# Two-layer hybrid encoder step on one core: the feed-forward stages take the first token group by itself, then the other two together, and the state-space input product opens with three blocks

## The chip, the cores and the metric

The kernel is one program on one core of a Trainium2 chip. The metric is the device time of one execution in microseconds (us), as the median of several runs. The core has a matmul engine (TensorE, PE in the profile, with its weight loads as PEld), three engines for elementwise work (VectorE, DVE; ScalarE, ACT; GpSimd, POOL), and SyncE (SP), which here only issues DMA transfers. Each engine runs its own list of instructions in order.

## The reference

1024 prompt tokens and 32 sample tokens pass through two layers in float32. Layer 0 mixes tokens by retention and forgetting attention, attends to 256 memory tokens, and ends in a feed-forward stage; layer 1 has a state-space mixer (S5) in place of the first step and then the same two. Every part is wrapped in norms:

```python
x = x + rmsnorm(part(rmsnorm(x) * w_pre)) * w_post
```

The feed-forward part, which the change rewrites, is

```python
h = relu(x @ w_up) ** 2      # 1024 -> 4096
y = h @ w_down               # 4096 -> 1024
```

and the S5 part begins with a product 1024 -> 1024 (`winc` in the kernel).

## The kernel before

Activations lie with features on the 128 partitions and tokens along the free axis. The 1056 tokens are three groups: 0 and 1 of 384 tokens, 2 of 288. A weight block is 128 outputs by 1024 inputs (512 KB).

**Products.** Each float32 product is three passes over exact splits of both sides, x = hi + lo and w = hi + lo (`mm3`): hi·hi, hi·lo, lo·hi. One block for one group is 8 inputs by 3 passes, 24 matmuls into one PSUM bank; three banks take turns (tag `mm`). All matmuls are recorded on line L72.

**Weights.** `wload` brings a block into `wst` (two buffers) by a DMA on the SP queue (L135), ScalarE copies it to `wh` (L139) and VectorE subtracts to get `wl` (L140); `wh` and `wl` have four buffers each. An optional offset gives these two a higher place in the order.

**Order of work.** The matmul engine's list is laid out by hand: `po.later(d, fn)` puts a piece off until d microseconds of products stand before it, and `po.tick()` lets due pieces in. The lists of the other engines are made by a scheduler from priorities; `tc.high_priority(offset=HP)` moves work ahead. Within `gemm` the evacuations of a block run in such a region.

**Feed-forward.** `mlp` goes over the 4096 hidden features in 8 chunks of 4 blocks. For each chunk it loads 4 up blocks, computes them for group 0, then 1, then 2 (`gemm`, evacuation `evac_up`: relu on ScalarE L1343, square on VectorE L1344, `ho` high part on ScalarE L1346, low part on GpSimd L1347), loads 4 down blocks, and adds the 8 outputs of each group to `Y` (first chunk a copy by ScalarE, then VectorE L1366). In the last chunk a group's outputs are squared and summed (`sumsq`: ScalarE L244, GpSimd L245) and `done(g)` starts the group's `update`. The third up block of the first chunk alone is loaded with the high offset HP.

**Update.** `update` closes each part for one group: the sums of squares become reciprocal norms (piece `c` on the matmul engine, put off by 3.2 us of products, then a broadcast `b`, put off by 3.0 us more), then for each of 8 feature tiles VectorE scales (`upd`, L273), adds the residual `xr` (L274; GpSimd takes some of them), ScalarE makes the high split `xh` (L201) and VectorE the low split `xl` (L202), and ScalarE squares it for the next norm (L244, added by GpSimd at L245). The next part's product for the group needs the splits of all 8. `r` is what the next stage scales its outcome by.

**What lies ahead of the change.** The output product of the memory attention ends with group 2 as well; its updates for groups 1 and 2 still run when the feed-forward begins with group 0. The end of layer 0's feed-forward meets the S5 input product in the same way; that product takes 2 blocks for all groups and then one block at a time (`gran`), and its states and outputs (`s5_block`) are put between the products by `po.later`.

Of the kernel before, what the change touches and what calls it, by code (L numbers as in the profile page):

```python
"""Hybrid retention / forgetting-attention / S5 streaming step on one core.

Activations are feature-major: features on partitions, tokens along the free axis; the 1024 prompt
tokens and the 32 sample tokens share every weight (token groups of 384, 384 and 256 + 32).
Large float32 products run as three float32r passes over exact splits x = hi + lo, w = hi + lo
(hi*hi + hi*lo + lo*hi); small products run in float32.
"""
# [9 lines left out]
F32 = mybir.dt.float32  # L17
F32R = mybir.dt.float32r
AF = mybir.ActivationFunctionType
# [4 lines left out]
NG = (384, 384, 288)  # L24
# [7 lines left out]
class _Order:  # L32
    """The tensor engine's program is laid out piece by piece; a piece that waits for other engines
    is put off until enough other products stand before it."""
# [29 lines left out]
def _body(tc, A):  # L64
# [21 lines left out]
    with es:  # L86
# [17 lines left out]
        # ---------------- constants  # L104
# [22 lines left out]
        # ---------------- helpers  # L127
# [20 lines left out]
        # evacuations can be held back until the pool they write to may be opened  # L148
# [14 lines left out]
        def gemm(blocks, load, rhs, evac, gran, done=None, post=None, lead=0, final=(0, 1, 2)):  # L163
            """blocks of 128 outputs, gran at a time for each token group; the first `lead` advance together"""
# [39 lines left out]
        def rstd_cols(acc, nt, scale, half=False, r=None, tag="rc", ps=None):  # L204
            """acc: [128, nt*128] partial sums of squares by partition -> [128, nt] reciprocal rms.
            With r, the columns summed up still lack a factor r^2."""
# [40 lines left out]
        def update(o, g, ys, acc, gpost, xres, xout, last=False, row=False, scale=1.0 / 1024, half=False, r=None):  # L247
            """x + rmsnorm(y) * g; o gets the split of the new x times the next norm's gain, and its
            reciprocal rms by token, in columns or along a row of all partitions"""
# [71 lines left out]
        # ---------------- memory keys and values of a layer (prompt)  # L321
# [63 lines left out]
        # ---------------- state-space layer: discretisation and per-group chunk matrices  # L385
# [8 lines left out]
        def s5_prepare(sp):  # L394
# [10 lines left out]
            # angles lambda_im*dt * (1, 8, 16, ..., 512), reduced to [-pi, pi]  # L405
# [20 lines left out]
            # powers a^0..a^8  # L426
# [19 lines left out]
            # input gains  # L446
# [26 lines left out]
            def group(f):  # L473
# [20 lines left out]
                def cmul(xr, xi, pr, pi, n, nm, neg):  # L494
                    """outer products over (power, channel): real part and (negated) imaginary part"""
# [839 lines left out]
        def mlp(l, X, done):  # L1335
            Y = [[None] * 8 for _ in range(3)]
            for c in range(8):
# [14 lines left out]
                for g in range(3):  # L1352
                    acc = acc_tile(NG[g]) if c == 7 else None
                    for o in range(8):
# [6 lines left out]
                        with tc.high_priority(offset=HP):  # L1361
# [5 lines left out]
                            if c == 7:  # L1367
                                sumsq(acc, Y[g][o], NG[g], o == 0, "sqa")
# [325 lines left out]
```

## Time and profile before

| what | value |
|---|---|
| device time, three runs | 3298.2, 3298.15, 3295.02 us; median 3298.15 us |
| span of the profiled execution | 3296.3 us |
| matmul engine busy | 3160.3 us (96%) |
| VectorE, ScalarE, GpSimd busy | 45%, 33%, 28% of the span |
| weight loads (`wh`, `wl`) | 252 |

The runs list no separate time for the profiled execution; its span is 1.85 us under the median of the runs. A wait of the matmul engine counts, a wait of another engine only where the matmul engine waits for it in turn. In the profile an arrow names the engine and line whose result ended an idle stretch. The granted clock is a share of full speed: 1.0 stands for 2.4 GHz and 0.5 for 1.2 GHz.

### The profile page before, as it was taken

Reading aid. Unit: us, or ns where it says so; the run is one execution under the profiler, and the core shown is the slowest. Engines: PE = TensorE matmul, PEld = TensorE weight load, DVE = VectorE, ACT = ScalarE, POOL = GpSimd, SP = SyncE. Lnnn points to the kernel's source line nnn. Section 1 sums busy time; section 2 is a strip of 40 time slices with the busy share of each in tenths; the row PEclk is TensorE's granted clock in tenths of the full one; section 3 lists DMA queues with packets and bytes.
Section 4 is the critical chain, followed back from the end, with each engine's and each line's share of the span. In section 5 each row is a group of like instructions: output and inputs, shape, how many; then the busy total and the mean of one; then the engine's idle time right before and its main releaser. Section 6 shows DMA issues by size and latency. Waiting matters only on the chain.

```text
span 3296.3 us, 50246 instructions
## 1 busy us (share of the span) xinstructions
PE 3160.3 (96%) x19972; PEld 3059.2 (93%) x19972; DVE 1495.2 (45%) x2756; ACT 1071.6 (33%) x2117; POOL 914.5 (28%) x1182
## 2 busy tenths in 40 slices
PE   7999999998999999999999888998999999999997
PEld 7899986688999999999999878998999999999997
DVE  8843566527435223332334797227426132233224
ACT  5212335425435322221124334225435321222212
POOL 4873431216115211111114442015106111111115
PEclk9999999999999999999999998999999999999998
DMA  5562244124114211110112677114124110111113
GB/s 157 156 194 70 62 137 128 38 58 141 52 42 128 65 42 52 52 47 31 52 52 74 204 241 222 57 52 141 49 66 124 52 47 32 52 52 52 39 58 99
DMA packets 176336, 285.71 MB, mean 87 GB/s; under 512 B 34027, under 2 KB 130508, under 8 KB 175972
## 3 DMA queue, kind: packets, MB, share of 16 engines
q1 hardware_dynamic: 132310, 215.02, 21.8%
q10 hardware_dynamic: 35328, 41.83, 3.8%
q0 software_dynamic: 8464, 25.66, 2.3%
q8 instruction: 157, 2.57, 0.3%
q14 instruction: 77, 0.63, 0.1%
HBM read 220.17 MB, written 66.39 MB: 87 GB/s over the span
## 4 chain that ended last, share of the span: by engine, by line
PE 77%; DVE 7%; POOL 6%; DMA 4%; issue 4%; ACT 2%; SPq 0%; DVEq 0%; ACTq 0%; POOLq 0%
PE mm L72 68%; PE a L72 4%; PE b L72 2%; POOL q L527 2%; POOL acc L245 2%; PE c L72 1%; DVE xl L202 1%; DVE wl L140 1%; DVE upd L274 1%; POOL ET L528 1%; DMA ed<-ET 1%; POOL ET L529 1%; DVE upd L273 1%; PE b L76 1%; DMA mt<-in_memt_dram 0%
## 5 line engine op out<-in xcount | busy, mean ns | idle before, releaser
L72 PE MATMUL mm<-xh,wh 128*128 128x384 f32 (+1 forms) x3168 | 1050.4, 332 | 6.5 <-ACT mo L382 3.7
L72 PE MATMUL mm<-xh,wl 128*128 128x384 f32 (+1 forms) x3168 | 1031.4, 326 | 7.4 <-DVE wl L140 7.3
L72 PE MATMUL mm<-xl,wh 128*128 128x384 f32 (+1 forms) x3168 | 1031.9, 326 | 1.2 <-DVE xl L202 1.2
L72 PE MATMUL mm<-ho,wh 128*128 128x384 f32 (+1 forms) x3456 | 822.9, 324 | 1.5 <-DVE y L1366 1.5
L72 PEld LDWEIGHTS mm<-xh,wh 128*128 128x128 f32 x3168 | 603.5, 190 | 13.8 <-issue 5.0
L72 PEld LDWEIGHTS mm<-xh,wl 128*128 128x128 f32 x3168 | 602.4, 190 | 9.0 <-DVE wl L140 9.0
L72 PEld LDWEIGHTS mm<-xl,wh 128*128 128x128 f32 x3168 | 603.5, 190 | 1.8 <-DVE xl L202 1.8
L72 PEld LDWEIGHTS mm<-ho,wh 128*128 128x128 f32 x3456 | 603.5, 188 | 1.8 <-DVE y L1366 1.8
L72 PE MATMUL mm<-ho,wl 128*128 128x384 f32 (+1 forms) x1728 | 558.2, 323 | 0.0
L1347 POOL TENSOR_TENSOR ho<-u,ho 128x384 fp32r<-128x384 f32 (+1 forms) x192 | 183.3, 955 | 1176.2 <-ACT ho L1346 1150.4
L140 DVE TENSOR_TENSOR wl<-wst,wh 128x1024 fp32r<-128x1024 f32 (+1 forms) x252 | 318.5, 1264 | 416.0 <-ACT wh L139 412.8
L139 ACT ACTIVATE wh<-wst 128x1024 fp32r<-128x1024 f32 (+1 forms) x252 | 266.5, 1059 | 708.9 <-PE mm L72 641.6
L245 POOL TENSOR_TENSOR acc<-acc,sq 128x384 f32<-128x384 f32 (+2 forms) x259 | 280.9, 1093 | 412.1 <-ACT sq L244 406.5
L1366 DVE TENSOR_TENSOR y<-y,mm 128x384 f32<-128x384 f32 (+1 forms) x336 | 174.3, 519 | 353.4 <-PE mm L72 353.2
L72 PEld LDWEIGHTS mm<-ho,wl 128*128 128x128 f32 x1728 | 325.5, 188 | 0.0
L1344 DVE TENSOR_TENSOR u<-u 128x384 f32<-128x384 f32 (+1 forms) x192 | 103.3, 538 | 409.7 <-ACT u L1343 409.7
L1343 ACT ACTIVATE u<-mm 128x384 f32<-128x384 f32 (+1 forms) x192 | 88.0, 458 | 313.8 <-PE mm L72 313.6
L1346 ACT ACTIVATE ho<-u 128x384 fp32r<-128x384 f32 (+1 forms) x192 | 95.7, 498 | 172.1 <-DVE u L1344 172.1
L1206 POOL TENSOR_SCALAR p<-p,mx 128x256 f32<-128x256 f32 (+1 forms) x72 | 36.7, 510 | 241.4 <-DVE mx L1205 138.8
L202 DVE SCALAR_TENSOR_TENSOR xl<-upd,gall,xh 128x384 fp32r<-128x384 f32 (+1 forms) x120 | 100.0, 834 | 5.1 <-ACT xh L201 4.8
L244 ACT ACTIVATE sq<-y 128x384 f32<-128x384 f32 (+1 forms) x126 | 61.9, 495 | 109.7 <-DVE y L1366 56.2
L72 PE MATMUL mm<-xo,wh 128*128 128x384 f32 (+1 forms) x384 | 92.1, 324 | 0.0
(427 smaller groups left out, 4132.9 us busy)
## 6 DMA issues: line engine op xcount, KB each, us to landing
wst<-in_wup_dram SPq DMA_DIRECT2D x64, 512.0 KB
wst<-in_wdn_dram SPq DMA_DIRECT2D x64, 512.0 KB
xs<-upd ACTq DMA_DIRECT2D x80, 192.0 KB
xr<-xs SPq DMA_DIRECT2D x80, 192.0 KB
wst<-in_wab_dram SPq DMA_DIRECT2D x20, 512.0 KB
wst<-in_wxk_dram SPq DMA_DIRECT2D x16, 512.0 KB
wst<-in_wxv_dram SPq DMA_DIRECT2D x16, 512.0 KB
wst<-in_wxq_dram SPq DMA_DIRECT2D x16, 512.0 KB
```

The source lines that it names most:

```text
L72: return nc.tensor.matmul(out, lhsT, rhs, **kw)
L139: act(wh[:, :n], st[:, :n], AF.Copy)
L140: vtt(wl[:, :n], st[:, :n], wh[:, :n].bitcast(F32), op=SUB)
L202: stt(l, src, gain, h.bitcast(F32), op0=MULT, op1=SUB)
L244: act(sq[:, :n], src, AF.Square)
L245: return gtt(acc[:, :n], acc[:, :n], sq[:, :n], op=ADD)
L527: gtt(o[:, :, :, :m], ET[:, :, :, :m], a_, op=MULT)
L1343: act(t, ps, AF.Relu)
L1344: vtt(t, t, t, op=MULT)
L1346: act(h, t, AF.Copy)
L1347: gtt(lo, t, h.bitcast(F32), op=SUB)
L1366: vtt(Y[g][o], Y[g][o], ps, op=ADD)
```

## The change

`mlp` no longer calls `gemm`. It first takes group 0 alone through the whole feed-forward, in 4 chunks of 8 up blocks and 8 down blocks (each down block of 1024 hidden features by 128 outputs is now half of two loads), and calls `done(0)`. Then it takes groups 1 and 2 together in 8 chunks of 4, as before. Every up and down weight is therefore read and split twice: 64 more loads of 512 KB in each layer, 128 in all. The number of matmuls stays the same. `hidden`, which replaces `evac_up`, is not in a high-priority region, and no up weight is loaded with HP any more. In S5 the first pass of the input product takes 3 blocks for all groups in place of 2.

```diff
         def mlp(l, X, done):
+            def hidden(ps, g, new):
+                n = NG[g]
+                t = npl.tile([128, 384], F32, tag="tmp", bufs=2, name="u")[:, :n]
+                act(t, ps, AF.Relu)
+                vtt(t, t, t, op=MULT)
+                h, lo = new(), new()
+                act(h, t, AF.Copy)
+                gtt(lo, t, h.bitcast(F32), op=SUB)
+                return h, lo
+            def up(w, x, g):
+                ps = bank()[:, : NG[g]]
+                for k in range(8):
+                    s = slice(k * 128, k * 128 + 128)
+                    mm3(ps, w[0][:, s], w[1][:, s], x[k][0], x[k][1], k == 0, k == 7)
+                    po.tick()
+                return ps
+            def down(ws, H, o, g):
+                ps = bank()[:, : NG[g]]
+                for k in range(len(H)):
+                    wh, wl = ws[k // 4]
+                    s = slice((k % 4) * 256 + (o % 2) * 128, (k % 4) * 256 + (o % 2) * 128 + 128)
+                    mm3(ps, wh[:, s], wl[:, s], H[k][0], H[k][1], k == 0, k == len(H) - 1)
+                    po.tick()
+                return ps
+            def gather(Y, o, g, ps, first, acc):
+                with tc.high_priority(offset=HP):
+                    if first:
+                        Y[o] = ytile(g)
+                        act(Y[o], ps, AF.Copy)
+                    else:
+                        vtt(Y[o], Y[o], ps, op=ADD)
+                    if acc is not None:
+                        sumsq(acc, Y[o], NG[g], o == 0, "sqa")
             Y = [[None] * 8 for _ in range(3)]
+            x = get(X, 0)
+            for c in range(4):
+                H = []
+                for b in range(8):
+                    w = wload(A["wup"][l, 8 * c + b], 8)
+                    H.append(hidden(up(w, x, 0), 0, lambda: otile(0)))
+                acc = acc_tile(NG[0]) if c == 3 else None
+                for s4 in range(4):
+                    ws = [wload(A["wdn"][l, 2 * c + j, s4], 4) for j in range(2)]
+                    for o in (2 * s4, 2 * s4 + 1):
+                        gather(Y[0], o, 0, down(ws, H, o, 0), c == 0, acc)
+            done(0, Y[0], acc)
             for c in range(8):
-                H = [[None] * 4 for _ in range(3)]
-                def evac_up(b, g, ps):
-                    n = NG[g]
-                    t = npl.tile([128, 384], F32, tag="tmp", bufs=2, name="u")[:, :n]
-                    act(t, ps, AF.Relu)
-                    vtt(t, t, t, op=MULT)
-                    h, lo = otile(g), otile(g)
-                    act(h, t, AF.Copy)
-                    gtt(lo, t, h.bitcast(F32), op=SUB)
-                    H[g][b] = (h, lo)
-                gemm(range(4), lambda b: wload(A["wup"][l, 4 * c + b], 8, HP if c == 0 and b == 2 else 0), lambda g, k: get(X, g)[k], evac_up, 4)
+                H = {1: [], 2: []}
+                ws = [wload(A["wup"][l, 4 * c + b], 8) for b in range(4)]
+                for g in (1, 2):
+                    for b in range(4):
+                        H[g].append(hidden(up(ws[b], get(X, g), g), g, lambda: otile(g)))
                 ws = [wload(A["wdn"][l, c, s], 4) for s in range(4)]
-                for g in range(3):
+                for g in (1, 2):
                     acc = acc_tile(NG[g]) if c == 7 else None
                     for o in range(8):
-                        wh, wl = ws[o // 2]
-                        ps = bank()[:, : NG[g]]
-                        for k in range(4):
-                            s = slice(k * 256 + (o % 2) * 128, k * 256 + (o % 2) * 128 + 128)
-                            mm3(ps, wh[:, s], wl[:, s], H[g][k][0], H[g][k][1], k == 0, k == 3)
-                            po.tick()
-                        with tc.high_priority(offset=HP):
-                            if c == 0:
-                                Y[g][o] = ytile(g)
-                                act(Y[g][o], ps, AF.Copy)
-                            else:
-                                vtt(Y[g][o], Y[g][o], ps, op=ADD)
-                            if c == 7:
-                                sumsq(acc, Y[g][o], NG[g], o == 0, "sqa")
+                        gather(Y[g], o, g, down([ws[o // 2]], H[g], o, g), c == 0, acc)
                     if c == 7:
                         done(g, Y[g], acc)
...
         close_after(left, X, (0, 1), s5_start)
-        gemm(range(8), lambda b: wload(A["winc"][b], 8, HP if b < 2 else 0), lambda g, k: get(X, g)[k], evac_u, lambda at: 2 if at == 0 else 1,
+        gemm(range(8), lambda b: wload(A["winc"][b], 8, HP if b < 2 else 0), lambda g, k: get(X, g)[k], evac_u, lambda at: 3 if at == 0 else 1,
              post=lambda b, g: s5_block(b, uts.pop(b)) if un[b] == 3 else None, final=(2, 0, 1))
         mem = memory_k(1, 2)
```

The rest of the difference takes out comments.

**VectorE at the start of layer 0's feed-forward, before.** `wl_12046` belongs to the third up weight, and `upd`, `xl` and `xr` here to groups 1 (384 wide) and 2 (288 wide) of the update; `upd_12174` is the first instruction of group 2's.

```order
L140 TENSOR_TENSOR wl_12046<-wst_12043,wh_12045 128x1024
L202 SCALAR_TENSOR_TENSOR xl_12090<-upd_12086,gall_81,xh_12089 128x384
L273 SCALAR_TENSOR_TENSOR upd_12152<-y_11741,gall_81,b_11928 128x384
L1344 TENSOR_TENSOR u_12114<-u_12114 128x384
L202 SCALAR_TENSOR_TENSOR xl_12131<-upd_12127,gall_81,xh_12130 128x384
L274 TENSOR_TENSOR upd_12152<-upd_12152,xr_12150 128x384
L273 SCALAR_TENSOR_TENSOR upd_12174<-y_11357,gall_81,b_12166 128x288
```

The fourth weight's `wl_12052` follows 10 rows below, in the middle of group 2's update.

**The same place after.** `wl_12200`, `wl_12277` and `wl_12362` belong to the third, fourth and fifth up weight.

```order
L273 SCALAR_TENSOR_TENSOR upd_12377<-y_12026,gall_81,b_12154 128x288
L274 TENSOR_TENSOR upd_12377<-upd_12377,xr_12375 128x288
L202 SCALAR_TENSOR_TENSOR xl_12323<-upd_12319,gall_81,xh_12322 128x288
L202 SCALAR_TENSOR_TENSOR xl_12345<-upd_12341,gall_81,xh_12344 128x288
L202 SCALAR_TENSOR_TENSOR xl_12381<-upd_12377,gall_81,xh_12380 128x288
L140 TENSOR_TENSOR wl_12200<-wst_12197,wh_12199 128x1024
L140 TENSOR_TENSOR wl_12277<-wst_12274,wh_12276 128x1024
L140 TENSOR_TENSOR wl_12362<-wst_12359,wh_12361 128x1024
L1342 TENSOR_TENSOR u_12267<-u_12267 128x384
L140 TENSOR_TENSOR wl_12413<-wst_12410,wh_12412 128x1024
```

The third and fourth weight's `wl` now stand behind the last `xl` of group 2's update. ScalarE's list agrees: `wh_12199` of the third weight stands behind `sq_12385`, the last square of that update. The matmul engine's list is unchanged up to the third block, and layer 1 has the same order at its feed-forward.

**ScalarE where the feed-forward turns from group 0 to groups 1 and 2, layer 0, after.** `u` are relus of the first up blocks of group 1 and then (288 wide) group 2, `ho` their high parts; `xh`, `xs` and `sq` belong to group 0's update, and `wh` to down weights. Before the change this place does not exist: group 0's update ran at the end of the feed-forward.

```order
L201 ACTIVATE xh_14811<-upd_14808,gall_81 128x384
L280 DMA xs207_138<-upd_14808 128x384
L244 ACTIVATE sq_14816<-upd_14808 128x384
L1344 ACTIVATE ho_14612<-u_14609 128x384
L1341 ACTIVATE u_14667<-mm_14616 128x384
L139 ACTIVATE wh_14909<-wst_14907 128x1024
L1344 ACTIVATE ho_14670<-u_14667 128x384
L1341 ACTIVATE u_14725<-mm_14674 128x384
L1341 ACTIVATE u_14783<-mm_14732 128x288
```

The first two relus of group 1 (`u_14561`, `u_14609`) stand ahead of group 0's update; the third (`u_14667`) stands behind all of it, 8 times `xh`, `xs` and `sq`. In layer 1, group 0's update is the last step and has no `xh` and no `sq`.

## Rows read from the trace of the kernel before

**Rows 1.** Windows: length, PE, PEld, DVE, ACT, POOL busy, PEclk, DMA, GB/s.

```profile
1000.00:1090.00 90.00, 84.16 (x494) 83.06 (x494) 59.13 (x87) 45.75 (x96) 58.09 (x57) 0.94 0.44 131
1090.00:1778.00 688.00, 688.00 (x4289) 688.00 (x4287) 195.45 (x304) 162.34 (x274) 93.08 (x98) 1.00 0.15 47
1778.00:1860.00 82.00, 70.93 (x416) 69.97 (x416) 64.20 (x110) 36.81 (x72) 54.77 (x59) 0.88 0.57 175
1860.00:2060.00 200.00, 171.41 (x1198) 167.30 (x1197) 165.67 (x213) 80.00 (x153) 68.82 (x68) 0.94 0.72 222
...
2500.00:2560.00 60.00, 54.32 (x319) 53.21 (x318) 49.78 (x74) 32.66 (x70) 46.26 (x45) 0.91 0.50 147
```

**Rows 2.** Page, costliest groups: busy, mean ns of one, idle before.

```profile
L1347 POOL TENSOR_TENSOR ho<-u,ho 128x384 fp32r<-128x384 f32 (+1 forms) x192 | 183.3, 955 | 1176.2 <-ACT ho L1346 1150.4
L140 DVE TENSOR_TENSOR wl<-wst,wh 128x1024 fp32r<-128x1024 f32 (+1 forms) x252 | 318.5, 1264 | 416.0 <-ACT wh L139 412.8
L139 ACT ACTIVATE wh<-wst 128x1024 fp32r<-128x1024 f32 (+1 forms) x252 | 266.5, 1059 | 708.9 <-PE mm L72 641.6
...
L1344 DVE TENSOR_TENSOR u<-u 128x384 f32<-128x384 f32 (+1 forms) x192 | 103.3, 538 | 409.7 <-ACT u L1343 409.7
L1343 ACT ACTIVATE u<-mm 128x384 f32<-128x384 f32 (+1 forms) x192 | 88.0, 458 | 313.8 <-PE mm L72 313.6
L1346 ACT ACTIVATE ho<-u 128x384 fp32r<-128x384 f32 (+1 forms) x192 | 95.7, 498 | 172.1 <-DVE u L1344 172.1
```

**Rows 3.** PE timeline, third and fourth up block of layer 0.

```profile
1063.75 0.34 PE L72 MATMUL mm<-xh,wh 128*128 128x384 f32 x1
...
1067.98 0.34 PE L72 MATMUL mm<-xh,wh 128*128 128x384 f32 x1
...
1071.45 0.51 PE L72 MATMUL mm<-xh,wl 128*128 128x384 f32 x1 [2.95 <-DVE wl L140]
```

**Rows 4.** DVE timeline inside and at the end of group 2's update, layer 0.

```profile
1069.38 2.01 DVE L140 TENSOR_TENSOR wl<-wst,wh 128x1024 fp32r<-128x1024 f32 x1
...
1075.49 0.55 DVE L1344 TENSOR_TENSOR u<-u 128x384 f32<-128x384 f32 x1
...
1080.69 1.16 DVE L1344 TENSOR_TENSOR u<-u 128x384 f32<-128x384 f32 x1
...
1083.20 0.61 DVE L202 SCALAR_TENSOR_TENSOR xl<-upd,gall,xh 128x288 fp32r<-128x288 f32 x1 [0.92 <-ACT xh L201]
```

**Rows 5.** ACT timeline, last square of that update.

```profile
1083.07 0.43 ACT L244 ACTIVATE sq<-upd 128x288 f32<-128x288 f32 x1
```

**Rows 6.** Windows after two stalls: length, PE busy, PEclk, DMA, GB/s.

```profile
1071.45:1078.20 6.75, 6.75 (x24) 0.52 0.62 188
61.40:64.80 3.40, 3.19 (x15) 0.51 0.60 171
```

**Rows 7.** Timeline in the middle of the feed-forward: one weight load issued.

```profile
1151.64 0.33 SPq L135 DMA_DIRECT2D wst<-in_wup_dram  x1
```

**Rows 8.** Window of that load: last columns are DMA share and GB/s.

```profile
1152.40:1154.60 2.20, 1.00 (x1) 1.00 0.79 238
```

**Rows 9.** SP, then ACT timeline: two loads beside other transfers.

```profile
501.61 2.53 SPq L135 DMA_DIRECT2D wst<-in_wout_dram  x2
...
507.16 1.06 ACT L139 ACTIVATE wh<-wst 128x1024 fp32r<-128x1024 f32 x1 [0.55 <-DMA wst<-in_wout_dram]
```

**Rows 10.** Waits of PE, 1778 to 1860 us: total, times, longest.

```profile
PE b L72 <- POOL rc L220: 5.6, 2, 4.4
PE c L72 <- POOL acc L245: 3.9, 2, 2.4
PE mm L72 <- DVE y L1366: 1.5, 1, 1.5
```

**Rows 11.** DVE timeline: update of group 0 after the feed-forward.

```profile
1782.80 1.14 DVE L273 SCALAR_TENSOR_TENSOR upd<-y,gall,b 128x384 f32<-128x384 f32 x2 [1.16 <-PE b L72]
...
1803.28 0.61 DVE L202 SCALAR_TENSOR_TENSOR xl<-upd,gall,xh 128x384 fp32r<-128x384 f32 x1
```

## The prediction

> **What bounds the kernel now.** I read the windows first, to see where the matmul engine is not full. Inside layer 0's feed-forward, from 1090 to 1778 us, it is busy for all 688.0 of 688 us at granted clock 1.00, while VectorE works 195.45 us, ScalarE 162.34 and the transfers take 0.15 of their engines [rows 1]. The number of matmuls does not change, so nothing can be gained there; only the places where the matmul engine waits can move. The same rows show three such places near the change. At the seam into the feed-forward (1000 to 1090 us) it loses 5.84 us and runs at 0.94; layer 1's seam (2500 to 2560 us) loses 5.68 of 60 us at 0.91 in the same way. From the end of layer 0's feed-forward into S5 (1778 to 1860 us) it loses 11.07 us at 0.88. In S5 (1860 to 2060 us) it loses 28.59 us, and there VectorE is busy 165.67 of 200 us, so that stretch is paced by VectorE and by chains through it more than by products.
>
> Next I read what each engine does in the first seam. The third up block starts at 1063.75 and the fourth at 1067.98; that one then waits 2.95 us for its `wl` and goes on at 1071.45 [rows 3]. So a block of 24 matmuls takes 4.23 us at full clock, and this seam is decided by when VectorE, busy with group 2's update, gets to a weight. After the wait the clock is granted at 0.52, close to 1.2 GHz, for 6.75 us; after the long wait at the program's start, work resumes with 3.40 us at 0.51 [rows 6]. A stall therefore costs its own length and about half of 3.4 to 6.75 us more: 1.7 to 3.4 us.
>
> **The change, part by part.**
>
> *First seam, both layers: the third up weight without its high offset.* The order shows its `wh` behind the last square of group 2's update on ScalarE and its `wl` behind the update's last `xl` on VectorE, while the matmul engine still asks for it at 1063.75. When does that update end? Before, its last `xl` ends at 1083.20 + 0.61 = 1083.81 [rows 4] and its last square at 1083.07 + 0.43 = 1083.50 [rows 5]. Out of its way on VectorE go the fourth weight's `wl` (2.01 us) and the squares of the third and fourth block (0.55 and 1.16 us), 3.72 us in all [rows 4]. If all of it came off, the last square would end at 1079.8; if GpSimd's sums, which ScalarE's squares wait for, pace it, nothing comes off and it stays at 1083.5. I take 1080.9, nearer the first, since the update is one chain through VectorE. Then come one `ho` that overlaps the end, `wh` (1.06 us) and `wl` (1.26 us) [rows 2], so the third block can start at about 1083.2. With 1.7 us of low clock and two blocks of 4.2 us the fourth block ends at 1083.2 + 1.7 + 8.4 = 1093.3. Before, 18 of its 22 remaining matmuls and 6 narrow ones lay in the 6.75 us up to 1078.20 [rows 6], and 4 more at 4.23/24 = 0.176 us make 1078.9. The loss is 14.4 us, and the fourth and fifth weight, split directly behind the third, wait for nothing more. At the ends: 10.7 us if the update's remaining work is also quickened by as much as left it (3.7 us, see the rivals), 19.5 us if nothing comes off, `wl` takes 2.01 us and the low clock costs 3.4. Layer 1 has the same order and the same idle time, so the term is 2 × 14.4 = **+28.8 us** (21 to 39).
>
> *Group 0 alone: end of the up blocks.* Before, the first down output of group 0 came after 8 up blocks of the other groups. Now it follows the last up block directly and reads its hidden part after 21 matmuls, 21 × 0.176 = 3.7 us. The chain relu, square, `ho`, low part takes 458 + 538 + 498 + 955 ns = 2.45 us [rows 2]. Alone it is covered. With the next weight's `wh` and `wl` (1.06 and 1.26 us) in front on both engines, which the order shows there, it is 4.77 us, 1.1 us too late. I take 0.7 us, nearer the second. It happens 4 times a layer: 8 × 0.7 = **+5.6 us** (0 to 10). A stall under 1 us gets no low clock from me: the only ones that lowered it in these rows lasted longer.
>
> *Turn from group 0 to the others.* In layer 0, ScalarE's relu of group 1's third up block stands behind all of group 0's update, and the matmul engine needs that bank back for its sixth block, 5 × 4.2 = 21 us after the turn. Before, group 0's update took from 1782.80 to 1803.89, 21.1 us, on VectorE [rows 11], with seven additions to `y` in between, which I take to be as long as a square of the same shape, 0.54 us [rows 2]. Without these and with two squares it needs some 18.5 us. It starts 3.2 + 3.0 us of products after the turn, so it ends near 25 us; the relu then comes some 4 us late. With 1.7 us of low clock that is **+6 us** (0 to 9; 0 if VectorE runs quicker beside an idle GpSimd). In layer 1 the update is the last step, without ScalarE's part, and I cost it at nothing.
>
> *Weights twice.* 128 more loads. In the group 0 stage each weight serves one block of 4.2 us, so each of the two `wst` buffers may take 8.4 us for a turn. Issued at 1151.64 [rows 7], a load alone moved its bytes by 1154.60 at 238 GB/s [rows 8], 2.96 us; with `wh` and `wl` the turn is 5.3 us. Per block VectorE has 1.26 + 0.54 = 1.8 us, ScalarE 1.06 + 0.46 + 0.50 = 2.0 us, GpSimd 0.96 us. All is hidden under 4.2 us of products, so the cost is 0; the cover goes if a load takes 6 us (rival W).
>
> *End of layer 0's feed-forward and S5.* Group 0's update no longer lies there, so the waits for `y` (1.5 us) and the first one for `acc` (3.9 − 2.4 = 1.5 us) go [rows 10], and with them about 3.5 us of half clock, 1.7 us: −4.7. The S5 product then has 9 instead of 6 blocks before the states begin; the states come no earlier, since group 2's norm comes last as before, but VectorE carries fewer additions beside them. I take −0.8 for that, together **−5.5 us**. The bounds are −20 (all that 1778 to 1860 us loses: 11.07 idle and 0.12 × 70.93 = 8.5 of clock [rows 1]) and +5 (three more blocks of the opening before the first states, part of them uncovered).
>
> **Sum.** 28.8 + 5.6 + 6 − 5.5 = +34.9 us on the profiled span of 3296.3 us, that is 3331.2; the median lies 1.85 us above that span, so the forecast is 3333.0 us. The smallest difference from no change that such runs can tell is about 0.2%, 6.6 us.
>
> **Rivals.**
>
> *T: the update is freed more than I took.* For: the same square takes 0.55 us in one place and 1.16 in another, and `wl` 2.01 us against a mean of 1.26 [rows 2, 4], so VectorE is being held up by neighbours, and GpSimd loses the low parts of two blocks as well. Against: GpSimd's sums and additions of the update stay. Then the seam costs 10.7 us a layer and the turn and the late hidden parts little: 3298.15 + 21.4 + 7 − 5.5 = 3321 us. The Trainium skill, "SBUF — State Buffer", "Who interferes with whom", says that a VectorE instruction with two inputs in SBUF and a GpSimd instruction that reads SBUF hold each other off. The trace agrees in kind (2.01 against 1.26 us), and by that rule this rival is the way it would go where GpSimd falls idle.
>
> *W: the weights bound the group 0 stage.* Two loads beside other transfers took from 501.61 to 507.16, 5.55 us [rows 9]. With `wh` 1.06 and a slow `wl` 2.01 and the issue of 0.33 us the turn is 8.95 us against 8.4, 0.55/2 = 0.27 us per weight, 128 weights: +35 us, 3368 us. Against it: these stages have hardly any other transfer, 0.15 of the transfer engines in use [rows 1], doubled still 0.3. The Trainium skill, "DMA: Bandwidth & Descriptors", "Bandwidth", asks for at least 1 MiB in a transfer and so speaks against reading 512 KB blocks twice; the 238 GB/s above show that the load alone stays within its turn.
>
> *F, the other side: the S5 stretch gives it back.* With group 0's update done early, the S5 states might start earlier and VectorE's queue might flow. From 1778 to 2060 us there are 39.7 us of idle matmul engine and about 8.5 + 0.06 × 171.41 = 18.8 us of lost clock [rows 1]. It decides when it gives back more than 34.9 − 6.6 + 5.5 = 34 of these 58 us in place of my 5.5; at 45 us the time is 3294 us. Against it: VectorE's 165.67 of 200 us in S5 stay, and they, not group 0, set the states' pace.
>
> **How the numbers follow.** The forecast as worked out 0.62; T 0.15; W 0.08; F 0.08; S5 or the turn worse than taken, near 3345 us, 0.07. The likeliest case alone spans 3322 to 3345. The range 3308 to 3354 leaves out W, most of F and a little more, about 2 in 10. Slower by over 0.2% (over 3304.7): all but F and a part of T, 0.88; within 0.2%: 0.05; faster: 0.07.
>
> **What would show it.** In the profile after: a wait of 18 to 20 us of the matmul engine for `wl` L140 at the third up block of each layer, with a granted clock near 0.5 behind it; in each layer four short waits for the low part (L1345) or `ho` (L1344) at the first down outputs of the group 0 stage, under 1 us each; one wait of about 4 us some 21 us after layer 0's turn, ended by ScalarE's relu (L1341); no wait for a weight transfer inside the group 0 stage; fewer waits between the feed-forward's end and S5, and S5 with VectorE as busy as now. I am wrong if the first wait is much shorter than 18 us, if `wst` ends waits of the matmul engine in the group 0 stage, or if 1778 to 2060 us shrinks by tens of us.

## The result

The changed kernel takes 3343.39 us (median of 4 runs, 3342.35 to 3347.34) against 3298.18 us before in the same session: a ratio of 1.0138, 95% interval 1.0124 to 1.0153. It is slower by some 45 us. The profiled execution spans 3340.6 us, 44.3 more than before.

First, windows of the kernel after over the places of [rows 1] (columns as there).

```profile
1053.81:1091.00 37.19, 20.21 (x92) 19.38 (x93) 28.96 (x42) 17.43 (x33) 19.96 (x19) 0.68 0.52 158
1090.00:1778.00 688.00, 682.98 (x4238) 681.15 (x4237) 262.01 (x352) 223.29 (x341) 109.41 (x111) 1.00 0.30 96
1826.00:1860.00 34.00, 30.94 (x175) 29.68 (x174) 30.93 (x57) 16.12 (x34) 22.56 (x25) 0.95 0.61 179
1860.00:2076.00 216.00, 173.67 (x1208) 169.86 (x1207) 164.23 (x208) 74.08 (x144) 72.98 (x73) 0.91 0.68 217
```

Inside the feed-forward the matmul engine is still all but full at clock 1.00 (682.98 of 688 us), with the transfers' share doubled from 0.15 to 0.30. The first seam, 37 us from the sums of group 1's norm on, holds only 20.21 us of products at clock 0.68. The opening of S5 (1826 to 1860 us) is fuller than before, but the rest of S5 keeps the matmul engine busy for 173.67 of 216 us, where VectorE has 164.23 us of work.

The matmul engine's timeline after: start, length, and in brackets the idle time ahead and what ended it.

```profile
1077.30 0.69 PE L72 MATMUL mm<-xh,wh 128*128 128x384 f32 x1 [15.62 <-ACT wh L139]
...
1079.66 0.69 PE L72 MATMUL mm<-xh,wl 128*128 128x384 f32 x1 [1.36 <-DVE wl L140]
...
1113.14 0.44 PE L72 MATMUL mm<-ho,wh 128*128 128x384 f32 x1 [0.51 <-POOL ho L1345]
...
1370.86 0.41 PE L72 MATMUL mm<-xh,wh 128*128 128x288 f32 x1 [2.79 <-ACT u L1341]
...
1825.79 0.29 PE L72 MATMUL mm<-ho,wl 128*128 128x288 f32 x1
...
1990.67 0.58 PE L72 MATMUL mm<-xmh,wh 128*128 128x256 f32 x1 [14.96 <-ACT wh L139]
...
2076.01 0.34 PE L72 MATMUL mm<-xh,wh 128*128 128x384 f32 x1
```

The third up block begins 15.62 us late, behind its weight's `wh`, and 1.36 us more go to `wl` (this answers to [rows 3]). The first down output of group 0's chunk waits 0.51 us for the low part, and three more like it follow in the layer with 0.53 each. At the turn 2.79 us are lost to the relu. Then comes a wait that nothing in the profile before announced: 14.96 us for the memory key product in S5. The two rows without brackets mark the last down product (1825.79) and the first wglu product (2076.01); the stretch between them, 250.2 us, is called the S5 stretch below.

ScalarE and VectorE at the seam after, answering to [rows 4, 5]:

```profile
1075.44 0.44 ACT L244 ACTIVATE sq<-upd 128x288 f32<-128x288 f32 x1
...
1076.20 1.99 ACT L139 ACTIVATE wh<-wst 128x1024 fp32r<-128x1024 f32 x2
...
1077.59 3.16 DVE L140 TENSOR_TENSOR wl<-wst,wh 128x1024 fp32r<-128x1024 f32 x2
```

The update's last square ends at 1075.88, `ho` overlaps, and the third and fourth weight's `wh` and `wl` follow at once.

The same marks of the S5 stretch before, with the wait at the same product:

```profile
1813.10 0.30 PE L72 MATMUL mm<-ho,wl 128*128 128x288 f32 x1
...
1979.12 0.39 PE L72 MATMUL mm<-xmh,wh 128*128 128x256 f32 x1 [4.43 <-DVE u L1438]
...
2049.37 0.34 PE L72 MATMUL mm<-xh,wh 128*128 128x384 f32 x1
```

There it lasts 236.3 us, and the key product waits 4.43 us, for a bank.

The time went here, between marks that both traces have (the sums `c` of group 1 at each layer's seam, the last down product, the broadcast that ends the norm behind wglu):

| stretch | before | after | difference |
|---|---|---|---|
| start to layer 0's seam | 1056.06 | 1053.81 | −2.25 |
| seam and feed-forward, layer 0 | 757.18 | 772.11 | +14.93 |
| S5 and wglu to its norm | 407.01 | 424.05 | +17.04 |
| to layer 1's seam | 303.34 | 301.87 | −1.47 |
| seam and feed-forward, layer 1, and end | 772.71 | 788.76 | +16.05 |
| sum | 3296.30 | 3340.60 | +44.30 |

The first row is no effect of the change: in the runs below this mark lies anywhere from 1052.6 to 1062.4 us, and run 2, whose program is the kernel before's up to there, has 1052.63. What sets it was not looked into.

### The profile page after: what moved, and what is told of

The parts are those of the page before. It is cut to its first block, busy times and chain, and to the rows that moved or that the text cites. A ratio compares the mean times of both kernels' runs of the same rounds, so it can differ in the third digit from the quotient of the medians.

```text
span 3340.6 us, 50900 instructions
## 1 busy us (share of the span) xinstructions
PE 3160.2 (95%) x19972; PEld 3053.9 (91%) x19972; DVE 1612.8 (48%) x2820; ACT 1196.8 (36%) x2245; POOL 920.4 (28%) x1182
## 5 line engine op out<-in xcount | busy, mean ns | idle before, releaser
L72 PE MATMUL mm<-xh,wh 128*128 128x384 f32 (+1 forms) x3168 | 1049.9, 331 | 45.1 <-ACT wh L139 31.2
L140 DVE TENSOR_TENSOR wl<-wst,wh 128x1024 fp32r<-128x1024 f32 (+1 forms) x380 | 475.0, 1251 | 648.9 <-ACT wh L139 645.6
L139 ACT ACTIVATE wh<-wst 128x1024 fp32r<-128x1024 f32 (+1 forms) x380 | 401.9, 1059 | 681.9 <-PE mm L72 591.4
L1371 DVE TENSOR_TENSOR y<-y,mm 128x384 f32<-128x384 f32 (+1 forms) x272 | 139.1, 512 | 251.3 <-PE mm L72 251.3
L201 ACT ACTIVATE xh<-upd,gall 128x384 fp32r<-128x384 f32 (+1 forms) x120 | 69.8, 584 | 72.3 <-DVE upd L274 64.5
```

The costliest lines, as they stand in the source:

```text
L72: return nc.tensor.matmul(out, lhsT, rhs, **kw)
L139: act(wh[:, :n], st[:, :n], AF.Copy)
L140: vtt(wl[:, :n], st[:, :n], wh[:, :n].bitcast(F32), op=SUB)
L201: act(h, src, AF.Copy, scale=gain)
L1371: vtt(Y[o], Y[o], ps, op=ADD)
```

## The experiments

Runs 1 to 4, 5 to 8, 9 and 10, 11, and 12 were each timed on one chip with runs of the kernel before between them (its medians there: 3297.42 to 3299.58 us). For each, the table gives the median, the ratio to the kernel before with its interval, and from the profile three stretches in us: layer 0's seam and feed-forward (from the sums `c` of group 0 to the start of the last down product), the S5 stretch, and layer 1's seam and feed-forward. The stretches are those of the one execution that was profiled, which can lie some us off the median (run 4's is its longest, 3353.99 us).

| run | median us | ratio (95%) | layer 0 | S5 | layer 1 |
|---|---|---|---|---|---|
| before | 3298.18 | | 775.2 | 236.3 | 768.7 |
| after | 3343.39 | 1.0138 (1.0124 to 1.0153) | 790.1 | 250.2 | 784.7 |
| 1. after, 2 blocks | 3328.66 | 1.0092 (1.0078 to 1.0107) | 789.4 | 237.0 | 785.6 |
| 2. before, 3 blocks | 3314.95 | 1.0051 (1.0038 to 1.0063) | 775.3 | 252.2 | 768.7 |
| 3. third weight raised | 3335.45 | 1.0112 (1.0097 to 1.0126) | 786.1 | 250.3 | 780.7 |
| 4. store moved | 3345.24 | 1.0139 (1.0123 to 1.0155) | 789.5 | 254.0 | 784.2 |
| 5. states first | 3353.34 | 1.0167 (1.0154 to 1.0180) | 790.2 | 258.6 | 784.3 |
| 6. third and fourth raised, 2 blocks | 3318.94 | 1.0059 (1.0048 to 1.0071) | 783.4 | 238.2 | 777.8 |
| 7. hidden raised | 3341.29 | 1.0131 (1.0118 to 1.0144) | 786.5 | 251.9 | 784.0 |
| 8. before, fourth raised | 3293.79 | 0.9989 (0.9979 to 0.9999) | 772.8 | 235.4 | 767.8 |
| 9. eight raised, 2 blocks | 3329.94 | 1.0099 (1.0084 to 1.0114) | 789.7 | 238.2 | 783.3 |
| 10. states sooner | 3336.08 | 1.0109 (1.0092 to 1.0126) | 789.5 | 244.9 | 784.8 |
| 11. all raised, 2 blocks | 3316.62 | 1.0047 (1.0034 to 1.0061) | 784.2 | 237.1 | 780.7 |
| 12. all raised, late norm, 2 blocks | 3301.17 | 1.0008 (0.9999 to 1.0017) | 773.5 | 238.2 | 771.4 |

### 1 and 2: the third opening block by itself

```diff
 # run 1, in after; run 2 is the reverse, in before
-gemm(range(8), ..., lambda at: 3 if at == 0 else 1,
+gemm(range(8), ..., lambda at: 2 if at == 0 else 1,
```

Run 1. 

> The changed kernel with the S5 product opening with 2 blocks again; the feed-forward stays as changed. Theory: the S5 stretch (from the end of layer 0's feed-forward to the wglu product) is 17 us longer after the change because of the third block alone, which puts the load of the last state block ahead of two memory tiles and a weight on SP's queue; with 2 blocks SP's list is as before there, so the time falls by 14 to 19 us, to 3324 to 3329. Rival: the stretch is longer because the rewritten feed-forward hands its groups over at other times; then the time stays within 3 us of 3343.

Run 2. 

> The kernel before with the S5 product opening with 3 blocks, nothing else. Theory: the third block alone costs its 13 to 17 us, so 3311 to 3315, with a wait of the matmul engine of over 10 us for the memory key product. Rival: it costs only beside the new feed-forward; then 3298 within 3.

Both came as the theory said in size: 15 us fewer in the one, 17.5 us more in the other, and in the table it is the S5 stretch alone that moves (237.0 and 252.2 us). The two parts of the change add up to within 4 us: 31.2 us for the feed-forward (3328.66 − 3297.42) and 17.5 for the third block alone in the kernel before, 48.8 against the 45.2 measured for both. So the size is shown to belong to the third block, whichever feed-forward stands ahead of it. The mechanism that the expectation names, SP's queue, was still open.

### 4: is it SP's queue?

In the trace after, SP issues the store of the last S5 block and right behind it two memory tiles, which the key product needs:

```profile
1982.85 0.34 SPq L1475 DMA_DIRECT2D ud<-u  x1
1983.28 1.28 SPq L348 DMA_DIRECT2D mt<-in_memt_dram  x2
```

```diff
-            dma(Ud[f][:, :, :], u)
+            (nc.gpsimd.dma_start if f == 7 else dma)(Ud[f][:, :, :], u)
```

> The changed kernel with one transfer moved: the store of the last S5 block (ud<-u) is issued by GpSimd in place of SP; SP's list is otherwise the same, and so are VectorE's and ScalarE's in that place. Theory: this transfer, which waits for VectorE until 1982.8 us, holds up the memory tiles and weights behind it on SP; without it they come some 11 us sooner and the wait of 15 us for the memory key product falls under 6 us; VectorE takes part of that back, so 6 to 11 us less in all, 3332 to 3337. Rival: VectorE's work paces the stretch and the transfer is only one more thing that is late; then under 3 us, 3340 to 3343.

The theory fell: 3345.24 us, and the S5 stretch did not shrink (254.0 us). The matmul engine's timeline of this run at the same product:

```profile
1994.01 0.55 PE L72 MATMUL mm<-xmh,wh 128*128 128x256 f32 x1 [5.93 <-DVE u L1468]
...
2003.60 0.58 PE L72 MATMUL mm<-xmh,wl 128*128 128x256 f32 x1 [8.82 <-DVE wl L140]
```

The wait is as long in sum as in the trace after, 5.93 + 8.82 = 14.75 us, now for VectorE. The tiles came sooner, but VectorE's list has the weight's `wl` behind the chain of the sixth states. SP was one of several that were late together, as the rival had it, though its 3340 to 3343 us were missed as well.

### 5 and 10: is it the place in the matmul engine's list?

With 2 opening blocks the list reads, from the sixth states on: 54 matmuls of the S5 product, outputs of the fifth block, states of the seventh, 9 matmuls, then 54 of the key product. With 3 blocks it reads: 12 of the S5 product, 54 of the key product, and only then states of the seventh and outputs of the fifth. The three-block opening uses up products early that later stood between the states, and the key product moves up to fill the place.

```diff
 # run 5: the states of the seventh block ahead of the key product
+        po.until(lambda: sd.get("n", 0) >= 7)   # counted in states()
         mem = memory_k(1, 2)
 # run 10: a shorter delay of the states
-        S1, S2 = 16.5, 20.0
+        S1, S2 = 9.0, 20.0
```

Run 5. 

> The changed kernel, with the states of the seventh S5 block put ahead of the memory key product in the matmul engine's list, where they stand with 2 opening blocks; the S5 product still opens with 3. Theory: with 3 opening blocks the key product stands ahead of those states, meets its operands some 15 us too early and holds up the states, whose chain through VectorE paces the stretch; with the states first the stretch from the feed-forward's end to the wglu product shrinks from 250 us to about 240, so 3331 to 3336. Rival: the third block's cost is in the lists of SP and VectorE (the key product's weights are split late); then the key product still waits over 8 us and the gain is under 4 us.

Run 10. 

> The changed kernel (3 opening blocks in S5) with the delay of the states behind their block cut from 16.5 to 9 us of products, which puts the seventh states and the fifth outputs ahead of the memory key product in the matmul engine's list, as they stand with 2 opening blocks. Theory: what the third block costs is this order, in which the key product stands ahead of work that is ready; the S5 stretch falls from 250 us to 234 to 240, so 3329 to 3335. Rival: VectorE's chain through the states sets the stretch whatever stands ahead of what; the stretch stays over 246 us.

Run 5 missed both: the S5 stretch grew to 258.6 us. The seventh states did start sooner (159.2 us after the last down product in place of 174.4), but the matmul engine had to wait 10.02 us for them, and later 7.45 us for the outputs of the sixth block:

```profile
1990.97 1.22 PE L72 MATMUL a<-U,Gm 128*128 128x132 f32 x4 [10.02 <-issue]
...
2026.44 0.81 PE L72 MATMUL b<-U,Tm 128*128 128x132 f32 x2 [7.45 <-ACT VC L1498]
```

Besides, 189 matmuls of the memory products instead of 147 were left behind the last outputs with nothing to stand beside. Run 10 puts both the seventh states and the fifth outputs ahead of the key product and starts the first states at 53.9 instead of 60.0 us; the stretch falls by 5.3 us to 244.9, between the two forecasts. So the order accounts for a part of the 14 us. What makes up the rest was not settled. In run 10 the key product waits only 1.03 us, so its late `wl`, the suspect after run 4, does not hold it up there; the long waits stand ahead of the seventh and the eighth states:

```profile
1983.44 1.22 PE L72 MATMUL a<-U,Gm 128*128 128x132 f32 x4 [6.53 <-DMA mt<-in_memt_dram]
...
2013.08 1.22 PE L72 MATMUL a<-U,Gm 128*128 128x132 f32 x4 [9.03 <-DMA yf<-yd]
```

Before the change these two waits were 4.28 us and none. There 123 matmuls of the key product stood ahead of the eighth states, in run 10 only 54, so the shorter delay brought the states too early in its turn. A list with 3 opening blocks and otherwise the order of before was not built.

### 3, 6, 9, 11, 12: the seam, one wait after the other

Each of these takes away what the matmul engine waited for last. Runs 6, 9, 11 and 12 have 2 opening blocks, and are to be read against run 1.

```diff
 # run 3: b == 2 with HP; run 6: b in (2, 3) with HP; run 9: all b with 600
-                    w = wload(A["wup"][l, 8 * c + b], 8)
+                    w = wload(A["wup"][l, 8 * c + b], 8, HP if c == 0 and b == 2 else 0)
 # runs 11 and 12: 600 where c == 0 and b > 1, and in hidden()
+                with tc.high_priority(offset=600):
                     act(t, ps, AF.Relu)
...
 # run 12 also, in update()
-                        po.later(L3, lambda: pre_scale(acc2))
+                        po.later(16.0 if gpost in (3, 9) else L3, lambda: pre_scale(acc2))
```

Run 3. 

> The changed kernel with the high offset on the third up weight of each layer again. Its wl then stands at the start of group 2's update on VectorE, but the fourth weight's wl stands among the last rows of that update (before the change: in the middle). Theory: the seam is decided by the last of the four weights; the third block fills 4 us of the wait and the fourth waits instead, so a gain of 4 to 6 us in each layer, 3332 to 3336. Rival: the missing offset on the third weight is the whole loss of the seam; then 12 to 14 us in each layer, about 3317.

It came as the theory said: 4.0 us less in each layer, 3335.45 us. The matmul engine's timeline of run 3, with the third block's wait and the fourth's:

```profile
1066.52 0.44 PE L72 MATMUL mm<-xh,wl 128*128 128x384 f32 x1 [2.25 <-DVE wl L140]
...
1080.08 0.69 PE L72 MATMUL mm<-xh,wl 128*128 128x384 f32 x1 [7.54 <-DVE wl L140]
```

The missing offset of the third weight was not the whole loss; the fourth weight took over.

Run 6. 

> The changed feed-forward with the high offset on the third and the fourth up weight of each layer, and the S5 product opening with 2 blocks. Both weights' wl now stand inside group 2's update on VectorE, as before the change. Theory: the seam falls back to what it cost before and only the small terms of the split stay: 2 x 2.1 us at the ends of group 0's up blocks, 2.8 us at the turn, less 4.7 us at the end of layer 0's feed-forward: 3296 to 3304. Rival: reading the weights twice costs elsewhere too; then over 3310.

This missed by some 15 us (3318.94): against run 1 each layer gained 6 to 8 us, not 14. The rival's number held, over 3310 us, but the cost was at the seam itself and not elsewhere. The timeline of layer 0 shows why:

```profile
1066.22 0.44 PE L72 MATMUL mm<-xh,wl 128*128 128x384 f32 x1 [2.24 <-DVE wl L140]
...
1072.06 0.44 PE L72 MATMUL mm<-xh,wl 128*128 128x384 f32 x1 [1.35 <-DVE wl L140]
...
1084.37 0.69 PE L72 MATMUL mm<-xh,wl 128*128 128x384 f32 x1 [7.18 <-DVE wl L140]
```

The third and fourth block there wait 2.24 and 1.35 us, and the fifth 7.18 us. Before the change four weights served twelve blocks, three groups of four, so no fifth was asked for until the update was over. With group 0 alone every block asks for a fresh weight, each 1.2 to 2.0 us on VectorE, in the stretch where VectorE carries the updates.

Run 9. 

> The changed feed-forward with a doubled high offset (600) on all 8 up weights of group 0's first chunk, and the S5 product opening with 2 blocks. In the run with the offset on the third and fourth weight alone, the fifth weight waited 7.2 us in their place: with group 0 alone every block needs a fresh weight, where before the change four weights served twelve blocks. Now the wl of the third to the sixth stand inside group 2's update on VectorE. Theory: no wait of over 3 us is left at the seam, and each layer's feed-forward falls from 765 and 760 us (third and fourth weight) by 8 to 11 us, to about the time of before: 3293 to 3302. Rival: VectorE has not the room beside the update, the wait only moves on to a later weight or into the update: over 3310.

No weight is waited for at the seam any more, and nothing is gained (3329.94 against run 1's 3328.66 us); the rival was right that the wait moves on. In its timeline the wait ahead of group 1's sums `c` has grown from 1.86 to 3.02 us, and behind it a block waits 9.94 us for the bank that a relu behind the update holds:

```profile
1060.96 1.23 PE L72 MATMUL c<-ones_c,acc 128*128 128x1 f32 x5 [3.02 <-POOL acc L245]
...
1090.66 0.69 PE L72 MATMUL mm<-xh,wh 128*128 128x384 f32 x1 [9.94 <-ACT u L1341]
```

Run 11. 

> The changed feed-forward with both the evacuation of the hidden features (relu, square, splits) and the up weights 3 to 8 of group 0's first chunk at the high offset 600, and the S5 product opening with 2 blocks. In the run with the weights alone raised no weight was waited for, but the third relu stood behind the update and the matmul engine waited 9.9 us for the bank. Theory: with both raised the update, which group 2's products need only 300 us later, gives way, no wait of over 3 us is left at the seam and the wait at the turn goes too; the feed-forward stages take about what they took before (757 and 750 us), 3293 to 3303. Rival: VectorE cannot hold both beside group 1's norm, and waits of the same sum appear for the norm's sums: over 3310.

Again the rival: 3316.62 us, and the waits are now for the sums `a` of the next norm, which the pushed back update brings late:

```profile
1075.16 1.01 PE L72 MATMUL a<-ones_c,acc 128*128 128x1 f32 x4 [5.56 <-POOL acc L245]
...
1091.89 0.80 PE L72 MATMUL a<-ones_c,acc 128*128 128x1 f32 x3 [3.14 <-POOL acc L245]
```

Run 12. 

> The run with weights and hidden features both raised, and with the next norm's sums of the updates ahead of the feed-forward (piece a) put off by 16 instead of 5.1 us of products. In that run the matmul engine no longer waited for a weight or a bank, but 5.6 and 3.1 us for these sums, which the update, now pushed back, brought late; the feed-forward needs them only at its end. Theory: the place where the matmul engine's list asks for the sums is the last thing that ties it to the update; put off, no wait of over 2 us is left from the norm's broadcast to the end of the seam, and the stages take 757 to 760 and 751 to 754 us: 3298 to 3305. Rival: VectorE's work in the seam is too much for the time in any order, and a wait of 5 us or more comes back in another place: over 3311.

Here it ends: 3301.17 us, ratio 1.0008 (0.9999 to 1.0017). The matmul engine's timeline has one longer wait for a weight ahead of the seam and one behind it, at the first down block:

```profile
1057.41 0.69 PE L72 MATMUL mm<-xh,wl 128*128 128x384 f32 x1 [2.81 <-DVE wl L140]
...
1097.69 0.75 PE L72 MATMUL mm<-ho,wh 128*128 128x384 f32 x2 [2.78 <-ACT wh L139]
```

The expectation of no wait over 2 us from the norm's broadcast to the end of the seam did not quite hold, as the second row shows. The stages took 773.5 and 771.4 us against 775.2 and 768.7 before. Nearly all of the feed-forward's loss was the order in which VectorE, ScalarE and the matmul engine's list were laid out at the seam, not the second reading of the weights: run 12 reads them twice as well. One thing stays open: the sums of the next norm were put off only in run 12, and what the kernel before would gain by that was not tried, so the comparison does not show that running group 0 ahead costs nothing at all.

### 7 and 8: two smaller ones

```diff
 # run 7, in hidden() of after: as in run 11, with offset HP and no weight raised
 # run 8, in the kernel before
-HP if c == 0 and b == 2 else 0
+HP if c == 0 and b in (2, 3) else 0
```

Run 7. 

> The changed kernel with relu, square and both splits of the hidden features in a high-priority region again (no offset on a weight). The third up weight's wl then comes at the start of group 2's update on VectorE, the fourth's behind it; at layer 0's turn the third relu of group 1 stands early in group 0's update. Theory: a gain of 4 to 5 us at each layer's seam and the 2.8 us of the turn: 3330 to 3334. Rival: what is moved ahead pushes group 2's update and the fourth weight back by as much; then 3338 to 3343.

Run 8. 

> The kernel before with the high offset on the fourth up weight too. Its wl then stands at the start of group 2's update on VectorE. Theory: the wait of 2.95 us and the low clock behind it (3.4 us) go in both layers, 12 us in all: 3285 to 3289. Rival: group 2's update ends later by the weight's 2 us and another wait takes the place; then 3292 to 3298.

Run 7, at 3341.29 us, lies in its rival's range of 3338 to 3343 us. Layer 0 gained 3.6 us, 2.8 of them at the turn, where the relu is no longer waited for; layer 1, which has no such wait, gained 0.7. At both seams the third block waited less, and the fourth waited 6.82 and 6.37 us for its weight, as the rival said. Run 8 is the fastest of all, 3293.79 us, by 0.1% (0.9979 to 0.9999). The wait for the fourth weight is gone in both layers; a wait of 2.13 us for the next norm's sums takes its place, so it gained 4.8 us, less than half of what was expected, and the rival (another wait takes the place, 3292 to 3298 us) was right.

## Why the prediction was right, and where it was not

The forecast of 3333.0 us with the range 3308 to 3354 holds the 3343.39 us, on the right side. That it does is in part luck: the case that came is the one that the prediction gave a chance of 0.07, "S5 or the turn worse than taken, near 3345 us", and one term was off by 17.8 us, with smaller errors the other way. Of its signs, the four short waits in each layer, the wait at the turn and the free weights came as named; the first wait, 15.62 us and 1.36 more for `wl`, was shorter than the 18 to 20 forecast. By its own terms:

**The seam, +14.4 us a layer: right in sum, by two errors that cancel.** Take the start of the fifth up block in layer 0. After, it is 1091.25, 37.4 us after `c` at 1053.81; before, it was 1079.20, 23.1 us after `c` at 1056.06. That is 14.3 us; the same marks in layer 1 give 13.0 us. But the update ended sooner than taken: the last square ended at 1075.88, which on the clock of before (2.25 us later) is 1078.1, not 1080.9, and the first two matmuls need only `wh`. So the third block began 23.5 us after `c` and not 27.1. What was saved there went again behind it: 1.36 us of waiting for `wl`, 0.6 us for a set of norm sums that the forecast left out, and the low clock. Windows after the stall in layer 0, after the one in layer 1 and after the turn's (length, PE busy, PEclk, DMA, GB/s) show

```profile
1077.30:1085.80 8.50, 7.14 (x21) 0.50 0.38 133
1085.90:1090.00 4.10, 4.10 (x27) 1.00 0.42 128
2575.33:2580.80 5.47, 4.11 (x12) 0.50 0.38 116
2580.90:2584.00 3.10, 3.10 (x20) 1.00 0.31 122
1370.80:1374.50 3.70, 3.64 (x27) 1.00 0.27 87
```

In layer 0 the matmul engine worked 7.14 us at 0.50, so 3.6 us were lost, where 1.7 was taken; in layer 1 it worked 4.11 us, so 2.1 were lost, which is about the difference between the layers. Rival T was therefore right about the update (by 2.8 us, not 3.7) and wrong about the total. The step "the fourth and fifth weight ... wait for nothing more" held for the kernel as changed, since both stand directly behind the third; run 6 shows that they were only hidden behind it.

**Group 0's late low part, +5.6 us: right in kind, 4.2 us in size.** Eight waits of 0.51 to 0.53 us. Both weights stood in front, as the order shows, but they ran in part beside the chain: from the end of the last up product at 1108.80 to the end of the low part at 1113.08 it took 4.3 us, between the 2.45 and the 4.77 us of the prediction, against 3.7 of cover.

```profile
1108.46 0.34 PE L72 MATMUL mm<-xh,wl 128*128 128x384 f32 x1
...
1112.08 1.00 POOL L1345 TENSOR_TENSOR ho<-u,ho 128x384 fp32r<-128x384 f32 x1 [3.14 <-ACT ho L1344]
```

**The turn, +6 us: place right, size 2.8 us.** The relu stands where the order shows it, and the matmul engine waited 2.79 us for it. The 1.7 us of low clock did not come: the window from 1370.80 has 1.00.

**Weights twice, 0: right.** Once the seam is over, the matmul engine has no wait of 0.3 us or more for a weight's `wh` or `wl` in either feed-forward, and run 12 with the same doubled loads is within 0.1% of before. Rival W is out; its 5.55 us from [rows 9] are also those of the first load alone, since the second weight's `wh` began only at 508.44. The Trainium skill, "DMA: Bandwidth & Descriptors", "Bandwidth", asks for at least 1 MiB in a transfer. That rule did not bear on the time here: the windows show the transfers' share at 0.30 of the feed-forward, so what the smaller blocks waste is not waited for.

**The end of layer 0's feed-forward, −4.7 us: right in kind, 6.2 us in size.** The two waits, 3.0 us together, are gone, and so is the low clock behind them. That was longer in the profile before than the 3.5 us taken, and cost 3.2 us:

```profile
1798.72:1805.50 6.78, 6.44 (x27) 0.50 0.52 169
```

With the sizes measured layer 0 comes to 14.3 + 4 × 0.53 + 2.8 − 6.2 = 13.0 us, against 14.93 in the table; layer 1, without the last two, to 13.0 + 2.1 = 15.1 us against 16.05, end included. About 0.6 us of what is left in layer 0 is a norm's broadcast that fell behind the mark before; the rest, about 1 us in each layer, belongs to no wait and was not traced.

**S5, −0.8 us: this step failed.** It read "the states come no earlier, since group 2's norm comes last as before, but VectorE carries fewer additions beside them". The states did come no earlier (60.0 us after the last down product, against 56.9 before). What the step did not ask is what the three more products had been covering before: they stood between the later states, and the memory key product that took their place was not ready. The stretch grew by 13.9 us and the wglu start by 3 more. The upper bound of +5 for this term and the one above together looked only at the opening; they came to about +11. Runs 1 and 2 show that the third block does this; runs 4, 5 and 10 that neither SP's queue nor the key product's place alone explains it.

So the time came out 10.4 us above the forecast: 17.8 us more from S5, 4.7 less from the two layers' seams and feed-forwards (31.0 us in the table against 28.8 + 5.6 + 6 − 4.7 = 35.7), and 3.7 less from the stretches that the change does not touch (−2.25 and −1.47), which leaves 9.4; the rest is that the median lies 2.8 us above the profiled span and not 1.85.

## What to carry to other kernels

Splitting a stage so that one group runs ahead alone changes how often fresh weights are asked for at its start, and that falls where the engine that prepares them still carries the stage before; look at the first blocks, not at the mean load. In a list laid out by hand, a block more at the front is a block less further back: name what it covered there and what will stand in its place. And when a wait is taken away, look for the next in the same list at once; here it took five edits (the third weight, the others, the relus, the norm's sums, two opening blocks) until the time of before was back.

## What the runs showed of the hardware that was not expected

After a wait of 15.62 us in layer 0 the granted clock stayed at 0.50 for 8.5 us, and after one of 15.63 us in layer 1 for 5.5 us, with a further wait of 1.36 us inside in both; the profile before has 3.40 us at the program's start and 6.75 us after a wait of 2.95 us [rows 6]. A wait of 2.79 us at the turn left it at 1.00. Neither the length of the low clock nor whether it came followed from the length of the wait in these rows.
